# Padded rows for the split x: where a matmul's moving operand begins

## The chip, the core and the metric

The kernel runs on one core of a Trainium2 chip. A core has five engines with queues of their own: TensorE (PE in the profile; its weight loads are PEld) multiplies matrices into PSUM, VectorE (DVE) and ScalarE (ACT) work elementwise, GpSimd (POOL) does a few elementwise and power operations, and SyncE (SP) issues transfers. On-chip memory (SBUF) has 128 partitions; an address below is a byte within a partition. The metric is the device time of one execution in microseconds (us); the time before is the median of three runs.

## What is computed

One layer of an encoder: the stream h is 16 meta tokens ahead of 1024 positions (T = 1040), width 1024. A combined projection of the normalized stream feeds a bidirectional retention with 4 heads and a windowed attention with 8 heads; both are gated, projected, merged, projected once more, normalized and added to h. Cut to what matters:

```python
u = _rms_norm(h, pre_w)
z = u @ w_in
rq, rk, rv, rg, aq, ak, av, ag, gr, ga = _split_in(z)
o_r = _bidirectional_retention(rq, rk, rv, lg_f, lg_b)
o_r = group_norm(o_r) * ret_nw * silu(rg)
y_r = o_r @ w_rb
o_a = _windowed_sink_attention(aq, ak, av, sink) * silu(ag)
y_a = o_a @ w_ab
mix = sigmoid(gr) * y_r + sigmoid(ga) * y_a
return h + _rms_norm(mix @ w_o, post_w)
```

## The kernel before

Everything that a matmul multiplies is split into a high part, rounded to float32r, and a low part, the remainder; `mm3` (line 73) makes a product of three matmuls, high by high, low by high and high by low. In the profile these are lines 75, 76 and 77.

**x.** The transposed stream times the norm's weight is kept split for the whole kernel in the four tiles `big[s][i]` (line 132): s = 0 is the high part, s = 1 the low part, i the upper or lower four of the eight rows k. A row k holds 128 of the 1024 input channels on the partitions and all T = 1040 columns, so rows lie 4160 bytes apart. Columns 0 to 15 are the meta tokens, columns 16 to 527 and 528 to 1039 the two halves. `proj` (line 136) uses x as the moving operand, in slices of 512 columns (`HALVES`, for queries) or 256 and 272 (`PIECES`, for keys), with the weights as the stationary one. `projT` (line 156) has x as the stationary operand and moves 256 columns of weights, for the values; for the 16 meta rows it uses `xm` instead, a packed copy that `pack_meta` makes. The profile names x `big` in all these places.

**Stages.** First comes the set-up: eight matmuls on zeros (`idle`, line 310) ahead of the first data, then the first head's query and key projection. Then four retention heads, with the next head's projections as filler between; decay tables `DT` are made a head ahead by `decay_table` (line 244) from `tabt`, in the loop over chunks c of `retention`. Attention follows, in 32 chunks, with query and key projections and some gate products (`pe`) as filler; its scores are combined with `mask` (line 1375 of the profile).

**The Strassen phases.** The gate projections (z, 16 units of 256 output channels) and the last three matrix products (r, a and o, 4 units each) use Strassen's scheme with seven products of half size. A product p of a unit u is 12 matmuls of 512 columns: three for each of four rows k. `PROD` gives its operands: the left one is a piece of the weights or a sum of pieces, made by `prepare` six products ahead; the right one stands in `B` for the whole phase. B11, B21, B22 and T1 are the quarters of `big` (the two halves of columns by the two halves of rows). T2, T3 and T4 are tiles of their own with rows of 2048 bytes, named T in the profile. Products 1, 2, 3 and 5 stream from `big`, products 4, 6 and 7 from T4, T2 and T3. Some products are made early and left out of a unit's list. Between two phases `refill` writes the next phase's right operands into the same places: `split_b` (line 917) with one operation on ScalarE and one on VectorE to a row, or `get_pre` (line 1090) with transfers of parts made earlier. T4 of the last phase comes by `get_pre` on SP.

The order of work on each engine is written out by hand through `fill`, `issue_after` and the tables of hooks, and set by the order in which the calls are recorded. The pools lay out SBUF from the bottom: tiles of the pool `keep` first, `big` among them.

Of the kernel before, what the change touches and what calls it, by code (L numbers as in the profile page):

```python
# [14 lines left out]
NM = 16  # L15
# [4 lines left out]
NH = 4  # L20
# [2 lines left out]
PIECES = [(0, 272), (272, 528), (528, 784), (784, 1040)]  # L23
HALVES = [(16, 528), (528, 1040)]
MW = 416
FILL = (9, 9, 7, 7, 7, 7, 6, 6), (7,) * 8, (7, 6, 6, 6, 6, 6, 6, 5), (5, 5, 5, 5, 5, 5, 8)
PRE = {u: (2, 3) if u > 5 else (2,) for u in range(2, 14)}

# [10 lines left out]
def block_kernel(ctx: ExitStack, tc: tile.TileContext, x0, xT, x, meta, w_in, w_rb, w_ab, w_out, post_w,  # L39
# [33 lines left out]
    def mm3(o, ah, al, bh, bl, first, last, free_group=False):  # L73
        kw = {"skip_group_check": True} if free_group else {}
        nc.tensor.matmul(o, ah, bh, start=first, stop=False, **kw)  # L75
        nc.tensor.matmul(o, al, bh, start=False, stop=False, **kw)  # L76
        latest[:] = [nc.tensor.matmul(o, ah, bl, start=False, stop=last, **kw).ins]  # L77
        return latest[0]
# [11 lines left out]
    def dve_lo(o, i, hi):  # L90
        return nc.vector.tensor_tensor(o, i, hi.bitcast(F32), ALU.subtract).ins  # L91
# [5 lines left out]
    rcol = keep.tile([P, 9], F32, name="rcol")  # L97
    rbc = keep.tile([P, T], F32, name="rbc")
    rnw = keep.tile([P, KT], F32, name="rnw")
    mhalf = keep.tile([P, 24], F32, name="mhalf")  # L100
    nc.vector.memset(mhalf, -0.5)

    def fetch_w(src, u):
# [25 lines left out]
            split(t, act)  # L129
        return w  # L130

    big = [[keep.tile([P, 4, T], R, name=f"big{i}_{s}") for i in range(2)] for s in range(2)]
    xh = [big[0][k // 4][:, k % 4] for k in range(KT)]
    xl = [big[1][k // 4][:, k % 4] for k in range(KT)]

    def proj(w, m0, a, b, name):
        wh, wl = w
# [6 lines left out]
        return t  # L144


    xm = wp.tile([P, KT, 2 * 32], R, name="xm")
    nc.vector.memset(xm.bitcast(F32), 0.0)

    def pack_meta():  # L150
        for i in range(2):
            for s in range(2):
                t = nc.vector.tensor_copy(xm[:, 4 * i:4 * i + 4, 32 * s:32 * s + NM], big[s][i][:, :, 0:NM].bitcast(F32))
        return t.ins

    def projT(w, c, name, mt=None):
# [39 lines left out]


    DT = ra.tile([P, NH, P], F32, name="DT")
    tabt = ra.tile([P, 3 * P], F32, name="tabt")
    mask = ra.tile([P, MW], F32, name="mask")  # L200
    warm = ra.tile([P, 1], F32, name="warm")
    neg, na, e, e2, s_, ss, acc, lg = (ra.tile([P, 8], F32, name=n) for n in (
        "neg", "na", "e", "e2", "s_", "ss", "acc", "lg"))
# [40 lines left out]
    def decay_table(hs):  # L244
        for h in hs:
            t = ra.tile([P, P], F32, tag="rw", bufs=3, name=f"dd{h}")
            nc.vector.tensor_scalar(t, tabt[:, 2 * P:3 * P], lg[:, 4 + h:5 + h], None, op0=ALU.mult)
            nc.vector.scalar_tensor_tensor(t, tabt[:, P:2 * P], lg[:, h:h + 1], t, op0=ALU.mult, op1=ALU.add)
            nc.scalar.activation(DT[:, h], t, AF.Exp)
# [17 lines left out]
    with tc.tile_pool(name="setup", bufs=1, reuse_waits="tile") as st:  # L267
# [32 lines left out]
            nc.sync.dma_start(xr[k], xT[k])  # L300
        nc.sync.dma_start(cr, rope[0])
        nc.sync.dma_start(sr, rope[1])
        nc.sync.dma_start(tabt, tab[:, MW:])
        w0 = tuple((lambda k, a, b, l=l: l[k // 4][:, k % 4, a:b]) for l in wt)


        idle = pj("idle")
        zeros = xm.rearrange("p k e -> p (k e)")
        for i in range(8):
            nc.tensor.matmul(idle, zeros[:, 0:P], zeros, start=True, stop=True)  # L310


        outs = [(P, a, b, t(f"pk0_{a}")) for (a, b), t in zip(PIECES, (pj, pj, p1, p3))]
# [68 lines left out]
        normed = nc.vector.tensor_tensor(kdr[:, 0:NH, 0], r2[:, 0:1].to_broadcast([P, NH]), dtab[:, 16:20], ALU.mult).ins  # L382
    nc.gpsimd.tensor_tensor(rcol, ms, mhalf[:, 0:9], ALU.pow)
    nc.vector.tensor_copy(ident, tabt[:, 0:P])
    nc.sync.dma_start(mask, tab[:, 0:MW])

    def row_factors():

# [52 lines left out]
    def retention(h, fill, begin=lambda: None):  # L441
# [98 lines left out]
        for c in range(9):  # L540
            if 0 < c < 8:
                stage1(c + 1)
            if c == 1:
                while pend:
                    pend.pop(0)()
            if h == 0 and c == 4:
                pins.extend((state["v"], state["vl"], state["S"]))
            if h == NH - 1 and c == 1:
                pre_fetch(6)
            if h == NH - 1 and c == 2:  # L550
                with tc.issue_after(state["vl"]):
                    pre_sums(6)
            if h == NH - 1 and c in (4, 6):
                fill(KT)
            if h == NH - 1 and 1 < c < 6:
                with tc.issue_after(state["vl"]):
                    turn_factors(*PIECES[c - 2])
            if h < NH - 1 and c == 4:
                with tc.issue_after(state["vl"]):
                    decay_table((h + 1,))  # L560
            if h == 1 and c == 2:
                row_factors()
            stage2(c)
# [329 lines left out]
    with follow(*latest):  # L893
# [5 lines left out]


    half = [slice(NM, NM + 512), slice(NM + 512, T)]
    B = {"B11": [big[s][0][:, :, half[0]] for s in range(2)], "T1": [big[s][0][:, :, half[1]] for s in range(2)],
         "B21": [big[s][1][:, :, half[0]] for s in range(2)], "B22": [big[s][1][:, :, half[1]] for s in range(2)]}
    PROD = {1: ("A11", "B11"), 2: ("A12", "B21"), 3: ("S4", "B22"), 4: ("A22", "T4"), 5: ("S1", "T1"),
            6: ("S2", "T2"), 7: ("S3", "T3")}
    free = ["pj"] * 3
    POST = {2: (0, 0), 7: (1, 1), 3: (0, 1), 4: (1, 0)}
    final = "o", 3, 4
    sub, mul, add = ALU.subtract, ALU.mult, ALU.add
# [5 lines left out]
        return gp.tile([P, 512], F32, tag="g", bufs=6, name=name)  # L915

    def split_b(n, k, src):
        h, l = B[n]
        nc.scalar.copy(h[:, k], src)
        dve_lo(l[:, k], src, h[:, k])  # L920

    class Phase:
        def __init__(self, nm, seq, load, post, fetch=None, apart=(), early=(), pre={}):
# [64 lines left out]
        def product(self, u, p):  # L988
            if (self.nm, u, p) == final:
                return self.last_product(u, p)  # L990
            st = self.u.setdefault(u, {})
            at = {1: "X", 6: "X", 7: "W" if u in self.apart else "X", 5: "Y", 3: "V" if u in self.early or (self.nm, u) == final[:2] else "Y", 2: "Z",
                  4: "W" if u in self.apart else "X"}[p]
            new = at not in st
            if new:
                b = free.pop(0)
                st[at] = bank(b, f"b{self.nm}{u}_{p}"), b
            t = st[at][0]
            h, l = self.ops.pop((u, p))
            bh, bl = B[PROD[p][1]]  # L1000
            for k in range(4):
                mm3(t, h[:, k], l[:, k], bh[:, k], bl[:, k], new and k == 0, k == 3, True)
            self.combine(u, p, st)

        def last_product(self, u, p):

            h, l = self.ops.pop((u, p))
            bh, bl = B[PROD[p][1]]
            o = self.u[u]["u3"]
            for a in (0, 256):  # L1010
                t = bank(free.pop(0), f"b{self.nm}{u}_{p}_{a}")
                s = slice(a, a + 256)
                for k in range(4):
                    mm3(t[:, 0:256], h[:, k], l[:, k], bh[:, k, s], bl[:, k, s], k == 0, k == 3)
# [74 lines left out]

    def get_pre(n):  # L1090
        for s in range(2):
            nc.sync.dma_start(B[n][s].bitcast(F32), pre_d[n][s])

    def get_sum(n):
        for k in range(4):
# [190 lines left out]
    def square(r, m2, c, o):  # L1286
        m1 = rows[r][2]
        jk = gtile(f"jk{r}_{c}")
        nc.scalar.activation(jk[:, 0:o.shape[1]], o, AF.Square, accum_out=m2[:, c:c + 1])
        if not m1:  # L1290
            m1.append(gp.tile([P, 1], F32, tag="ms1", bufs=6, name=f"ms1_{r}"))
            nc.vector.tensor_scalar(m1[0], m2[:, c:c + 1], 0.25 / D, EPS, op0=ALU.mult, op1=ALU.add)
        else:
            nc.vector.scalar_tensor_tensor(m1[0], m2[:, c:c + 1], 0.25 / D, m1[0], op0=ALU.mult, op1=ALU.add)
# [43 lines left out]
    def attention():  # L1338
# [4 lines left out]
        def stage1(hp, n):  # L1343
# [19 lines left out]
            for e_ in range(2):  # L1363
                hd = 2 * hp + e_
                if (hp, e_, i) not in aqs:
                    split_q(hp, e_, i)
                a_, b_ = (t[:, o0:o0 + P] for t in aqs[hp, e_, i])
                s = p2(f"ps{hd}_{n}")
                mm3(s[:, 0:wid], a_, b_, kh[:, start:start + wid], kl[:, start:start + wid], True, True)
                if n == 0:  # L1370
                    if hp:
                        raw[e_] = aw.tile([P, 401], F32, tag=f"raw{e_}", bufs=1, name=f"raw{hd}")
                    nc.vector.tensor_copy(raw[e_][:, 0:1], nsink[:, hd:hd + 1])
                p = pp[:, e_]
                nc.vector.tensor_tensor_reduce(raw[e_][:, 1:1 + wid], s[:, 0:wid], mask[:, mo:mo + wid], -SCALE,  # L1375
                                               nsink[:, hd:hd + 1], ALU.add, ALU.min, nm_[:, e_:e_ + 1])
# [169 lines left out]
    free.extend(["p1", "p1", "p2", "p2", "p3"])  # L1546
    yp, gp, yt = (ctx.enter_context(tc.tile_pool(name=n, bufs=1, reuse_waits="tile")) for n in ("yp", "gp", "yt"))
    for n in ("T2", "T3", "T4"):
        B[n] = [yt.tile([P, 4, 512], R, name=f"{n}{s}")[:, :, :] for s in range(2)]
    for n in ("T2", "T3", "T4"):  # L1550
        get_sum(n)
        next(steps)
# [79 lines left out]
```

## Time and profile before

| | us |
|---|---|
| median of three runs | 1053.21 (1052.04 to 1054.81) |
| the profiled execution | 1053.81 |
| its span, first to last instruction | 1051.7 |

The stages, with the busy time of TensorE and VectorE and the mean busy share of the 16 DMA engines in each stretch:

| stretch, us | what runs | PE | DVE | DMA |
|---|---|---|---|---|
| 5 to 29 | set-up, head 0's projection | 23.77 | 19.77 | 1.02 |
| 90 to 331 | retention heads | 241.00 | 181.81 | 0.30 |
| 331 to 440 | attention, first part | 108.96 | 81.70 | 0.57 |
| 440 to 555 | attention, second part | 114.12 | 86.23 | 0.58 |
| 555 to 620 | z phase, first part | 64.86 | 59.80 | 0.80 |
| 740 to 803 | z phase, last part | 63.00 | 56.23 | 0.58 |
| 803 to 881 | r phase | 77.65 | 71.11 | 0.60 |
| 881 to 960 | a phase | 78.77 | 64.88 | 0.86 |
| 960 to 1045 | o phase | 85.00 | 56.34 | 0.56 |

Matmuls overlap: the next starts while the one before is still in the array, so a matmul's duration in the profile (about 0.39 us at 512 columns) is longer than the distance to the next start. What a stretch of matmuls costs is read from the starts. In a row of a view by groups stand the line, the engine, the operation, the tiles written and read, the shape, the count, and then the busy time in us, the mean duration in ns and the idle time ahead. Buffer numbers are left out of the names.

### The profile page before, as it was taken

The numbers are of one execution on the slowest core, as the hardware profiler recorded it, in microseconds if no ns is written. First come the engines' busy times: TensorE is split into PE (matmuls) and PEld (weight loads), VectorE is DVE, ScalarE is ACT, GpSimd is POOL, SyncE is SP. The second block draws the span as 40 slices with busy tenths as digits, with TensorE's granted clock in tenths as the row PEclk, the third lists the DMA queues.
The fourth block names the chain that finished last, engine by engine and source line by source line (L and its number), as shares of the span: only waits on it lengthen the run. The fifth ranks groups of instructions, "written<-read, shape, count | busy, mean of one in ns | idle before, by whom it ended". The sixth has DMA issues, their size and how long they took to land. (4 is left out here: it accounts for less than half of the span.)

```text
span 1051.7 us, 17222 instructions
## 1 busy us (share of the span) xinstructions
PE 1040.9 (99%) x5880; PEld 905.4 (86%) x5880; DVE 838.3 (80%) x1788; ACT 506.5 (48%) x1127; POOL 228.4 (22%) x338
## 2 busy tenths in 40 slices
PE   9999999999999999999999999999999999999997
PEld 8998999989989888988888888778888788788886
DVE  6876758768875777777769988998899899778665
ACT  5631432423423566665667544555556446334443
POOL 3445244243242333443310000000000000111032
PEclk9999999999999999999999999999999999999999
DMA  9433223243231466666549678999935747789464
GB/s 347 176 86 87 65 46 83 69 92 98 77 92 61 101 176 182 174 183 168 161 154 347 188 255 318 306 321 345 394 106 170 256 154 233 224 232 315 126 120 80
DMA packets 96758, 188.43 MB, mean 179 GB/s; under 512 B 10944, under 2 KB 35552, under 8 KB 95856
## 3 DMA queue, kind: packets, MB, share of 16 engines
q1 hardware_dynamic: 79120, 162.89, 46.1%
q0 software_dynamic: 10176, 14.73, 9.4%
q10 hardware_dynamic: 7376, 9.73, 2.6%
q8 instruction: 46, 0.75, 0.3%
q14 instruction: 40, 0.33, 0.1%
HBM read 124.32 MB, written 57.68 MB: 173 GB/s over the span
## 5 line engine op out<-in xcount | busy, mean ns | idle before, releaser
L1247 POOL DMA_DIRECT2D mx_d<-c1a x4 | 3.6, 890 | 398.7 <-DVE c1a L1238 379.7
L76 PE MATMUL bz<-T,llz 128*128 128x512 f32 x192 | 75.0, 391 | 0.0
L77 PE MATMUL bz<-T,lhz 128*128 128x512 f32 x192 | 74.8, 389 | 0.0
L75 PE MATMUL bz<-T,lhz 128*128 128x512 f32 x192 | 74.5, 390 | 0.2 <-DVE u2z L1028 0.2
L76 PE MATMUL pv<-wh,big 128*128 128x256 f32 x256 | 73.2, 286 | 0.0
L75 PE MATMUL pv<-wh,big 128*128 128x256 f32 x256 | 73.2, 286 | 0.0
L77 PE MATMUL pv<-wl,big 128*128 128x256 f32 x256 | 73.1, 286 | 0.0
L76 PE MATMUL bz<-big,llz 128*128 128x512 f32 x176 | 69.7, 396 | 0.1
L75 PE MATMUL bz<-big,lhz 128*128 128x512 f32 x176 | 68.8, 395 | 0.6 <-ACT lhz L943 0.5
L77 PE MATMUL bz<-big,lhz 128*128 128x512 f32 x176 | 69.3, 394 | 0.0
L1378 ACT ACTIVATE p<-raw,nm 128x401 f32<-128x401 f32 (+1 forms) x64 | 38.3, 600 | 32.8 <-DVE nm L1375 31.5
L1388 POOL TENSOR_SCALAR p<-p,den 128x400 f32<-128x400 f32 (+1 forms) x60 | 37.6, 684 | 68.4 <-DVE den L1381 64.8
L75 PE MATMUL paq<-big,wh 128*128 128x512 f32 x128 | 51.8, 404 | 0.0
L76 PE MATMUL paq<-big,wl 128*128 128x512 f32 x128 | 50.8, 397 | 0.0
L77 PE MATMUL paq<-big,wh 128*128 128x512 f32 x128 | 50.4, 394 | 0.0
L75 PEld LDWEIGHTS pv<-wh,big 128*128 128x128 f32 x256 | 48.2, 188 | 0.4
L76 PEld LDWEIGHTS pv<-wh,big 128*128 128x128 f32 x256 | 48.2, 188 | 0.4
L77 PEld LDWEIGHTS pv<-wl,big 128*128 128x128 f32 x256 | 48.3, 189 | 0.3
L91 DVE TENSOR_TENSOR wl<-wr,wh 128x1024 fp32r<-128x1024 f32 x28 | 34.8, 1247 | 10.9 <-POOL wh L88 6.8
L75 PEld LDWEIGHTS bz<-T,lhz 128*128 128x128 f32 x192 | 36.0, 188 | 8.4 <-DVE u2z L1028 0.6
L76 PEld LDWEIGHTS bz<-T,llz 128*128 128x128 f32 x192 | 36.0, 188 | 8.0 <-DVE llz L91 0.3
L77 PEld LDWEIGHTS bz<-T,lhz 128*128 128x128 f32 x192 | 36.1, 188 | 7.6
(616 smaller groups left out, 3603.5 us busy)
## 6 DMA issues: line engine op xcount, KB each, us to landing
wrz<-in_w_in_dram SPq DMA_DIRECT2D x32, 512.0 KB, 6.2
wr<-in_w_in_dram SPq DMA_DIRECT2D x29, 512.0 KB, 3.8
we<-in_w_in_dram SPq DMA_DIRECT2D x16, 512.0 KB, 4.2
tg<-tg_d SPq DMA_DIRECT2D x32, 256.0 KB, 5.0
T<-preT SPq DMA_DIRECT2D x6, 1024.0 KB, 8.2
e<-e ACTq DMA_DIRECT2D x20, 256.0 KB, 2.9
e<-e SPq DMA_DIRECT2D x20, 256.0 KB, 4.9
xn<-in_x_dram SPq DMA_DIRECT2D x8, 512.0 KB, 9.2
```

The source lines that it names most:

```text
L75: nc.tensor.matmul(o, ah, bh, start=first, stop=False, **kw)
L76: nc.tensor.matmul(o, al, bh, start=False, stop=False, **kw)
L77: latest[:] = [nc.tensor.matmul(o, ah, bl, start=False, stop=last, **kw).ins]
L91: return nc.vector.tensor_tensor(o, i, hi.bitcast(F32), ALU.subtract).ins
L1247: nc.gpsimd.dma_start(d, to, accum_op=ALU.add)
L1378: last["exp"] = nc.scalar.activation(p[:, 0:1 + wid], raw[e_][:, 0:1 + wid], AF.Exp, scale=-1.0, bias=nm_[:, e_:e_ + 1], accum_out=den[:, ...
L1388: nc.gpsimd.tensor_scalar(pt[e_][:, 0:wid], pt[e_][:, 0:wid], den[:, e_:e_ + 1], 1.0, op0=ALU.mult, op1=ALU.mult)
```

## The change

- The four tiles of x become two, `big[s]`, with eight rows of LEFT + T = 1088 columns, 4352 bytes. x stands in columns 48 to 1087; columns 0 to 47 of each row are padding. `mhalf` grows by 64 bytes, which moves the start of `big`.
- T4 loses its fourth row (k = 3). It goes into `margins`: the padding and the 16 meta columns of all eight rows, 8 pieces of 64 columns. `right(n, s, k)` returns the operand and a function that views a flat row as 8 by 64. `product`, `last_product` and `split_b` go through it; `get_pre` brings the row by a transfer of its own for each part.
- `mask` takes the buffer of `tabt` and is loaded in retention head 2, behind the last decay table, instead of in the set-up.
- `xm` has 48 columns a row instead of 64, and the idle matmuls stream 384 columns instead of 512.
- `ms1` has 4 buffers instead of 6.

```diff
+LEFT = 48
...
-    mhalf = keep.tile([P, 24], F32, name="mhalf")
+    mhalf = keep.tile([P, 40], F32, name="mhalf")
...
-    big = [[keep.tile([P, 4, T], R, name=f"big{i}_{s}") for i in range(2)] for s in range(2)]
-    xh = [big[0][k // 4][:, k % 4] for k in range(KT)]
-    xl = [big[1][k // 4][:, k % 4] for k in range(KT)]
+    big = [keep.tile([P, KT, LEFT + T], R, name=f"big{s}") for s in range(2)]
+    xh, xl = ([b[:, k, LEFT:LEFT + T] for k in range(KT)] for b in big)
...
-    xm = wp.tile([P, KT, 2 * 32], R, name="xm")
+    xm = wp.tile([P, KT, 32 + NM], R, name="xm")
...
-    tabt = ra.tile([P, 3 * P], F32, name="tabt")
-    mask = ra.tile([P, MW], F32, name="mask")
+    tabt = ra.tile([P, MW], F32, tag="tb", bufs=1, name="tabt")
...
-            nc.tensor.matmul(idle, zeros[:, 0:P], zeros, start=True, stop=True)
+            nc.tensor.matmul(idle[:, 0:KT * (32 + NM)], zeros[:, 0:P], zeros, start=True, stop=True)
...
-    nc.sync.dma_start(mask, tab[:, 0:MW])
+    mask = []
+
+    def load_mask():
+        mask.append(ra.tile([P, MW], F32, tag="tb", bufs=1, name="mask"))
+        nc.sync.dma_start(mask[0], tab[:, 0:MW])
...
             if h < NH - 1 and c == 4:
                 with tc.issue_after(state["vl"]):
                     decay_table((h + 1,))
+                if h == NH - 2:
+                    load_mask()
...
-    B = {"B11": [big[s][0][:, :, half[0]] for s in range(2)], "T1": [big[s][0][:, :, half[1]] for s in range(2)],
-         "B21": [big[s][1][:, :, half[0]] for s in range(2)], "B22": [big[s][1][:, :, half[1]] for s in range(2)]}
+    B = {n: [big[s][:, 4 * i:4 * i + 4, LEFT + half[j].start:LEFT + half[j].stop] for s in range(2)]
+         for n, i, j in (("B11", 0, 0), ("T1", 0, 1), ("B21", 1, 0), ("B22", 1, 1))}
...
+    margins = [b[:, :, 0:LEFT + NM] for b in big]
+
+    def right(n, s, k):
+        if n == "T4" and k == 3:
+            return margins[s], lambda t: t.rearrange("p (a c) -> p a c", a=KT)
+        return B[n][s][:, k], lambda t: t
...
     def split_b(n, k, src):
-        h, l = B[n]
-        nc.scalar.copy(h[:, k], src)
-        dve_lo(l[:, k], src, h[:, k])
+        (h, as_), (l, _) = (right(n, s, k) for s in range(2))
+        nc.scalar.copy(h, as_(src))
+        dve_lo(l, as_(src), h)
...
             for k in range(4):
-                mm3(t, h[:, k], l[:, k], bh[:, k], bl[:, k], new and k == 0, k == 3, True)
+                (bh, as_), (bl, _) = (right(PROD[p][1], s, k) for s in range(2))
+                mm3(as_(t), h[:, k], l[:, k], bh, bl, new and k == 0, k == 3, True)
...
+                    if k == 3:
+                        c = slice(a // 64, a // 64 + 4)
+                        mm3(t[:, 0:256].rearrange("p (a c) -> p a c", a=4), h[:, k], l[:, k], bh[:, c], bl[:, c],
+                            False, True)
...
         for s in range(2):
-            nc.sync.dma_start(B[n][s].bitcast(F32), pre_d[n][s])
+            m = B[n][s].shape[1]
+            nc.sync.dma_start(B[n][s].bitcast(F32), pre_d[n][s][:, 0:m])
+            if m < 4:
+                d, as_ = right(n, s, m)
+                nc.sync.dma_start(d.bitcast(F32), as_(pre_d[n][s][:, m]))
...
-            m1.append(gp.tile([P, 1], F32, tag="ms1", bufs=6, name=f"ms1_{r}"))
+            m1.append(gp.tile([P, 1], F32, tag="ms1", bufs=4, name=f"ms1_{r}"))
...
-        B[n] = [yt.tile([P, 4, 512], R, name=f"{n}{s}")[:, :, :] for s in range(2)]
+        B[n] = [yt.tile([P, 3 if n == "T4" else 4, 512], R, name=f"{n}{s}")[:, :, :] for s in range(2)]
```

More of the change, by code (lines that the diff above doesn't have):

```diff
@@ L152, in pack_meta @@
             for s in range(2):
-                t = nc.vector.tensor_copy(xm[:, 4 * i:4 * i + 4, 32 * s:32 * s + NM], big[s][i][:, :, 0:NM].bitcast(F32))
+                t = nc.vector.tensor_copy(xm[:, 4 * i:4 * i + 4, 32 * s:32 * s + NM],
+                                          big[s][:, 4 * i:4 * i + 4, LEFT:LEFT + NM].bitcast(F32))
         return t.ins
@@ L302, in block_kernel @@
         nc.sync.dma_start(sr, rope[1])
-        nc.sync.dma_start(tabt, tab[:, MW:])
+        nc.sync.dma_start(tabt[:, 0:3 * P], tab[:, MW:])
         w0 = tuple((lambda k, a, b, l=l: l[k // 4][:, k % 4, a:b]) for l in wt)
@@ L999, in product @@
             h, l = self.ops.pop((u, p))
-            bh, bl = B[PROD[p][1]]
             for k in range(4):
-                mm3(t, h[:, k], l[:, k], bh[:, k], bl[:, k], new and k == 0, k == 3, True)
+                (bh, as_), (bl, _) = (right(PROD[p][1], s, k) for s in range(2))
+                mm3(as_(t), h[:, k], l[:, k], bh, bl, new and k == 0, k == 3, True)
             self.combine(u, p, st)
@@ L1007, in last_product @@
             h, l = self.ops.pop((u, p))
-            bh, bl = B[PROD[p][1]]
             o = self.u[u]["u3"]
@@ L1013, in last_product @@
                 for k in range(4):
-                    mm3(t[:, 0:256], h[:, k], l[:, k], bh[:, k, s], bl[:, k, s], k == 0, k == 3)
+                    (bh, _), (bl, _) = (right(PROD[p][1], e_, k) for e_ in range(2))
+                    if k == 3:
+                        c = slice(a // 64, a // 64 + 4)
+                        mm3(t[:, 0:256].rearrange("p (a c) -> p a c", a=4), h[:, k], l[:, k], bh[:, c], bl[:, c],
+                            False, True)
+                    else:
+                        mm3(t[:, 0:256], h[:, k], l[:, k], bh[:, s], bl[:, s], k == 0, False)
                 with tc.high_priority(200):
@@ L1374, in stage1 @@
                 p = pp[:, e_]
-                nc.vector.tensor_tensor_reduce(raw[e_][:, 1:1 + wid], s[:, 0:wid], mask[:, mo:mo + wid], -SCALE,
+                nc.vector.tensor_tensor_reduce(raw[e_][:, 1:1 + wid], s[:, 0:wid], mask[0][:, mo:mo + wid], -SCALE,
                                                nsink[:, hd:hd + 1], ALU.add, ALU.min, nm_[:, e_:e_ + 1])
```

## The prediction

> **What bounds the kernel now.** I read the page first for how full each engine is, then the list of what TensorE waited for, then the matmuls one by one in the order of time.
>
> ```profile
> PE 1040.9 (99%) x5880; PEld 905.4 (86%) x5880; DVE 838.3 (80%) x1788; ACT 506.5 (48%) x1127; POOL 228.4 (22%) x338
> ...
> PE idle L310 <- DVE warm L208: 1.5, 1, 1.5
> PE bz L75 <- ACT lhz L943: 0.5, 1, 0.5
> ```
>
> TensorE (PE) is busy 1040.9 of 1051.7 us. In the list of waits (in all, times, longest, in us) the longest is the 1.5 us ahead of the first instruction; the next is 0.5 us. So no other engine and no transfer holds the path for long: the time is the sum of the distances from one matmul's start to the next one's. A busy share can't say whether these distances are as short as they can be, since the ends are modelled; the starts can. The view in order of time, TensorE alone (start, duration in us, line), gives whole products of 12 matmuls, of which I keep the first row and the row that follows the last:
>
> ```profile
> 613.83 0.39 PE L75 MATMUL bz<-T,lhz 128*128 128x512 f32 x1
> ...
> 616.55 0.39 PE L75 MATMUL bz<-T,lhz 128*128 128x512 f32 x1
> ...
> 638.73 0.39 PE L75 MATMUL bz<-T,lhz 128*128 128x512 f32 x1
> ...
> 641.47 0.39 PE L75 MATMUL bz<-T,lhz 128*128 128x512 f32 x1
> ...
> 789.28 0.39 PE L75 MATMUL bz<-big,lhz 128*128 128x512 f32 x1
> ...
> 789.96 0.40 PE L75 MATMUL bz<-big,lhz 128*128 128x512 f32 x1
> ...
> 790.66 0.40 PE L75 MATMUL bz<-big,lhz 128*128 128x512 f32 x1
> ...
> 791.37 0.40 PE L75 MATMUL bz<-big,lhz 128*128 128x512 f32 x1
> ...
> 792.07 0.39 PE L75 MATMUL bz<-big,lhz 128*128 128x512 f32 x1
> ```
>
> The same work, with the same 128x512 shape, the same kind of stationary operand and no wait in it, takes 2.72 and 2.74 us when its moving operand comes from a T tile, and 2.79 us when it comes from big. The last five rows show where the difference sits: a product runs over four rows k of its operand, three matmuls to a row (L75 to L77). Row 0 takes 0.68 us, as a T row does (2.72 / 4); rows 1 to 3 take 0.70, 0.71 and 0.70 us.
>
> What sets row 0 of big apart is its address. A row of a big tile is T = 1040 columns, 4160 bytes, which is 64 modulo 256; in the built program the tiles begin at 64 modulo 256, and both halves begin 64 bytes (or 64 + 2048) into a row. So rows 0 to 3 begin at 128, 192, 0 and 64 modulo 256. All T rows are 2048 bytes from a base at 128. One start of the four, 128, is the fast one; that 0 is no better than 64 I take from the rows as they are, without a reason for it.
>
> The groups by shape (count, busy us, mean ns) show that this holds in every stage; of each I keep line 77, whose counts are those of 75 and 76 too:
>
> ```profile
> L77 PE MATMUL bz<-T,lhz 128*128 128x512 f32 x192 | 74.8, 389 | 0.0
> L77 PE MATMUL bz<-big,lhz 128*128 128x512 f32 x176 | 69.3, 394 | 0.0
> L77 PE MATMUL paq<-big,wh 128*128 128x512 f32 x128 | 50.4, 394 | 0.0
> L77 PE MATMUL pe<-big,weh 128*128 128x512 f32 x80 | 31.5, 394 | 0.0
> L77 PE MATMUL ba<-big,lha 128*128 128x512 f32 x64 | 25.2, 394 | 0.0
> L77 PE MATMUL pq<-big,wh 128*128 128x512 f32 x48 | 18.9, 394 | 0.0
> ```
>
> 394 ns for every group on big, 389 on T.
>
> **The change, part by part.** *The rows (term 1).* Rows become 1088 columns, 4352 = 17 x 256 bytes, the tiles begin at 128 modulo 256, and the data begin 48 columns in: every 512-column start is then 128 modulo 256, as in T. The big groups count 176 + 128 + 80 + 3 x 64 + 48 + 16 = 640 on each of three lines, 1920 matmuls (br and bo have ba's 4 units x 4 products on big x 4 rows = 64; head 0's queries 2 halves x 8 rows = 16, as each of the three heads in pq). The four Strassen phases (bz, br, ba, bo) have 1104 of them, 92 products. From the rows above a big product takes 2.79 us, a T product 2.73 on the mean of two: 0.06 x 92 = 5.5 us. The projections (paq, pe, pq) have 816, 68 times twelve. Two such twelves of head 3:
>
> ```profile
> 215.56 0.39 PE L75 MATMUL pq<-big,wh 128*128 128x512 f32 x1
> ...
> 218.36 0.39 PE L75 MATMUL pq<-big,wh 128*128 128x512 f32 x1
> ...
> 221.85 0.39 PE L75 MATMUL pq<-big,wh 128*128 128x512 f32 x1
> ...
> 224.63 0.39 PE L75 MATMUL pq<-big,wh 128*128 128x512 f32 x1
> ```
>
> 2.80 and 2.78 us, again 2.79: 0.06 x 68 = 4.1 us. Together 9.6 us. The least that these rows allow is 2.78 - 2.74 = 0.04 for all 160, 6.4 us; the most 2.80 - 2.72 = 0.08, 12.8 us. The group means give 5 ns x 1920 = 9.6 us as well. With 2.785 us as the typical product (between 2.78 and 2.79) it is 0.055 x 160 = 8.8; I take 9.2, half way.
>
> The Trainium skill, "TensorE: Matmul & The Clock Gate" (section "Wait — 56ns, not 53.3ns?"), gives the distance of warm matmuls as columns / 2.4 GHz plus some 2.5 ns, 215.7 ns at 512 columns, with no term for an address. The trace's 2720 / 12 = 227 ns and 2790 / 12 = 232 ns agree neither with it nor with each other; by that rule term 1 is nothing.
>
> *Matmuls of 256 columns and less.* Their starts move too (the chunks of the retention's tiles from 192 to 0 modulo 256, the weights as moving operands stay). Two groups of four in a row, on different operands:
>
> ```profile
> 301.69 0.28 PE L76 MATMUL pa<-vh,sl 128*128 128x256 f32 x1
> ...
> 302.17 0.28 PE L77 MATMUL pa<-Slf,qh 128*128 128x256 f32 x1
> ...
> 1042.02 0.28 PE L75 MATMUL bo<-T,lho 128*128 128x256 f32 x1
> ...
> 1042.50 0.28 PE L76 MATMUL bo<-T,llo 128*128 128x256 f32 x1
> ```
>
> 0.48 us for four in both, although the first begin at 192 (vh, Slf) and the second at 128. So at 256 columns the start shows no price, and I take nothing.
>
> *T4's fourth row in the margins (term 2).* Product 4 now streams row 3 of T4 as 8 pieces of 64 columns, 4352 bytes apart: 28 units x 3 = 84 matmuls (in the last one two half-width triples). No row of the trace has a moving operand in pieces. Bounds: at best a piece costs nothing, since each begins at 128 modulo 256 and the output stays one run of 512. At worst a new piece restarts the stream as a new matmul does: two 256-column matmuls take 0.24 us against 0.227 for one of 512, 13 ns a restart, 7 restarts x 84 x 13 = 7.6 us. In between lies the price of one slow start, 5 ns a matmul, 0.4 us; I take that, because the piece has neither a new stationary operand nor a new output.
>
> *The warm-up (term 3).* xm shrinks from 64 to 48 columns a row, so the eight idle matmuls stream 384 columns instead of 512.
>
> ```profile
> 1.48 3.78 PE L310 MATMUL idle<-xm 128*128 128x512 f32 x8 [1.48 <-DVE warm L208]
> 5.49 0.77 PE L75 MATMUL pq<-big,w 128*128 128x512 f32 x1 [0.23 <-ACT big L330]
> 6.05 0.63 PE L76 MATMUL pq<-big,w 128*128 128x512 f32 x1
> 6.48 0.41 PE L75 MATMUL pk<-big,w 128*128 128x272 f32 x1
> ...
> 7.08 0.40 PE L75 MATMUL pq<-big,w 128*128 128x512 f32 x1
> ```
>
> Until 6.48 us a 512-column matmul takes 0.43 us (6.05 to 6.48) and shows 0.63 us of duration; at 7.08 it shows the 0.40 of all later rows. So full speed comes about 5.0 us after the first idle matmul. The idle ones now end 8 x 0.43 / 4 = 0.86 us sooner, while the first real one still waits for ScalarE's high part of x at 5.49: TensorE has that much more of a hole. If full speed comes later by the hole, half of it is lost, 0.4 us; at worst the 5.0 us run again at half speed, 2.5 us; at best nothing. I take 0.4. The Trainium skill (same page, "What's actually happening") has the clock decided per free-running window of 3.41 us of activity; a window missed would cost an estimated 1.7 us, inside these bounds, and no run here shows the window.
>
> *The mask.* It now uses tabt's buffer and is asked for on SP behind VectorE's last read of the tables.
>
> ```profile
> L248 DVE SCALAR_TENSOR_TENSOR dd<-tabt,lg,dd x4: 330/347/349, 43.1 to 189.8; 128x128 f32<-128x128 f32 x4
> 186.63 5.62 SPq L580 DMA_DIRECT2D oTr_d<-ost  x2
> L1375 DVE CUSTOM_DVE_ANT_0 raw<-ps,mask,nsink x64: 491/630/636, 336.9 to 545.7; 128x400 f32<-128x400 f32 x48, 128x272 f32<-128x272 f32 x16
> ```
>
> The last table read ends at 190.1 us. Queued behind the new wait on SP is the second of these two output chunks, which goes at about 192 by itself (186.63 + 5.62, less its own issue), and behind that the weights of the next head; SP therefore stands there anyway. The first reader of the mask comes at 336.9, 145 us later. Cost nothing; without that cover, the attention's first chunk would wait for one landing.
>
> *T4's reload ahead of phase o* becomes four transfers, two of them in pieces of 256 bytes.
>
> ```profile
> 959.05 0.39 PE L75 MATMUL bo<-big,lho 128*128 128x512 f32 x1
> 967.59 0.79 SPq L1092 DMA_DIRECT2D T<-preT  x2
> ```
>
> Phase o begins at 959.05 and T4 is the operand of its 13th product: 12 x 2.73 us later, at 992 at the earliest, 24 us after the request. Two more issues of 0.4 us and pieces of 256 bytes don't fill that. Nothing; a reload later than that would hold this product. The instructions' order on every engine stays that of before, but for a few dozen matmuls of the first 25 us; TensorE gets 19 more waits on its own finished matmuls, each over 100 matmuls old, so they are met on arrival. The two ms1 buffers fewer add no wait of VectorE that comes late. Nothing for these.
>
> *What the others make of a faster TensorE (term 4).* Busy us of the engines in a stretch (PE, PEld, DVE, ACT, POOL, then clock and DMA share):
>
> ```profile
> 680.00:740.00 60.00, 59.72 (x259) 48.01 (x258) 55.45 (x92) 31.14 (x54) 0.00 (x0) 1.00 0.97 340
> ```
>
> In this stretch of the z phase VectorE is 92% busy and the DMA engines 97%. TensorE gets about 1% shorter there, which both can still follow on the mean. At worst all that z gains is lost: 44 products x 0.06 = 2.6 us; I take 0.4.
>
> *Sum:* 9.2 - 0.4 - 0.4 - 0.4 = 8.0 us less. The profiled execution took 1053.81 us (span 1051.7, 2.1 around it), which gives 1045.8; it lies 0.6 above the median of the three runs, 1053.21, so the median becomes 1045.2.
>
> **The rivals.** (a) *The others eat part of it:* z's gain is lost to VectorE and DMA (2.6), and the clock comes as late as its bound (2.5): 9.2 - 0.4 - 2.6 - 2.5 = 3.7 less, 1049.5. For it: 92% and 97%; against it: no wait of TensorE above 0.5 us in the list. (b) *The pieces cost 13 ns a restart:* 9.2 - 7.6 - 0.8 = 0.8 less, 1052.4. For it: the price that a new matmul has; against it: nothing else is new in a piece. (c) *The start isn't the cause:* something else sets row 0 and T apart, and the time stays, 1053.2; this is also what the skill's formula gives. Against it: row 0 of big shares only its start with T, not the row's length nor its tile; T's rows 1 to 3 are as fast as its row 0. (d) *Slower:* a piece restarts the stream at the price that short matmuls have.
>
> ```profile
> 500.85 0.62 PE L1405 MATMUL pt<-ident,p 128*128 128x128 f32 x4
> ```
>
> Four of 128 columns take 0.62 us with a tail of some 0.27, 0.115 each, where a quarter of 227 ns is 57: 58 ns a restart, 588 restarts, 34 us: 1053.2 - 8.4 + 34 = 1079. It decides from 14 ns a restart, where it has eaten the 8.4 us of the rest. Those are transposes of another type of data, which speaks against it.
>
> **How the numbers follow.** The forecast has 0.75, with a range of its own of 1042.6 to 1048; (a) 0.08, (b) 0.06, (c) 0.04, (d) 0.07. The range must leave out (b), (c) and (d) at most: 1042.6, where term 1 is nearly 11 us and nothing is given back, to 1050.5, which holds (a). This kernel's runs differ by 0.3% (3.2 us), so that is what can be told from no change: faster by more 0.83 (forecast and (a)), within it 0.10 ((b) and (c)), slower 0.07 ((d)).
>
> **What would show it.** Right: the big groups of 512 columns at 389 to 390 ns, big products 2.72 to 2.74 us from start to start, all four rows alike; TensorE's waits as short as before. Term 2: the third line of T4's row 3 in the bz products at 0.23 us to the next start, or longer by the restarts. Term 3: the idle group at about 2.9 us for eight, and the row from which 512 columns show 0.40. Term 4: new waits on VectorE or DMA between 555 and 803 us. I am wrong if the big groups stay at 394, or if product 4 is longer than the others.

## The result, and the profile after

| | before | after |
|---|---|---|
| median of 10 runs each, us | 1053.66 (1052.04 to 1055.84) | 1050.81 (1049.72 to 1053.56) |
| the profiled execution, us | 1053.81 | 1049.72 |
| its span, us | 1051.7 | 1047.6 |

The ratio is 0.9975, with an interval of 0.9964 to 0.9986: faster by 2.85 us of median, where the prediction had 8.0. The profiled execution of after is the fastest of its ten runs, so the two traces are 4.1 us apart and the medians 2.85.

The line of busy times on the page of after:

```profile
PE 1032.9 (99%) x5880; PEld 906.8 (87%) x5880; DVE 838.9 (80%) x1788; ACT 505.6 (48%) x1127; POOL 227.1 (22%) x338
```

TensorE is busy 8.0 us less than before (1040.9), but the span is only 4.1 us shorter, so part of what it gained it now stands idle. Where, is read in three views. First the order of time on TensorE (start, duration, line), in the z phase; `mm3` is now on lines 76 to 78, and of each product of 12 I keep the first row:

```profile
735.50 0.39 PE L76 MATMUL bz<-big,lhz 128*128 128x512 f32 x1
...
738.22 0.39 PE L76 MATMUL bz<-T,lhz 128*128 128x512 f32 x1
...
740.94 0.39 PE L76 MATMUL bz<-T,lhz 128*128 128x512 f32 x1
...
742.98 0.39 PE L76 MATMUL bz<-big,lhz 128*128 128x512 f32 x1
...
743.66 0.39 PE L76 MATMUL bz<-big,lhz 128*128 128x512 f32 x1
```

A product on big (735.50), one on T (738.22) and one on T4 (740.94, its last three matmuls on the margins from 742.98) all take 2.72 us; the three on the margins take 0.68, a quarter of it. So x streams as fast as T, and the 8 pieces of T4's fourth row cost nothing. The groups by shape say the same of every stage:

```profile
L78 PE MATMUL bz<-big,lhz 128*128 128x512 f32 x192 | 74.2, 389 | 0.0
...
L78 PE MATMUL pv<-wl,big 128*128 128x256 f32 x256 | 73.5, 287 | 0.0
...
L78 PE MATMUL paq<-big,wh 128*128 128x512 f32 x128 | 50.1, 392 | 0.0
...
L78 PE MATMUL ba<-big,lha 128*128 128x512 f32 x68 | 26.5, 389 | 0.0
...
L78 PE MATMUL pq<-big,wh 128*128 128x512 f32 x48 | 18.7, 390 | 0.0
```

The groups of 512 columns on big went from 394 to 389 in the Strassen phases and to 390 to 392 ns in the projections. The second row is one of 256 columns: pv's high-by-low line had 286 ns before and has 287 now. That looks like nothing, but there are 1040 such matmuls of pv and pav, and the starts show it better. Here are the first and the 25th matmul of 24 in a row in the first values of head 0, before and then after:

```profile
30.61 0.28 PE L75 MATMUL pv<-wh,big 128*128 128x256 f32 x1
...
33.45 0.28 PE L75 MATMUL pv<-wh,big 128*128 128x256 f32 x1
```

```profile
30.77 0.28 PE L76 MATMUL pv<-wh,big 128*128 128x256 f32 x1
...
33.64 0.28 PE L76 MATMUL pv<-wh,big 128*128 128x256 f32 x1
```

24 of them took 2.84 us and now take 2.87. From all starts of the two traces (stalls, more than 25 ns over the median of their kind, left out), the mean distance went from 118.0 to 119.2 ns for the 1040 of pv and pav, from 117.6 to 119.3 for the 432 of pk and pak, and from 118.6 to 119.2 for the 740 of retention and attention on their own tiles: 1.3 + 0.7 + 0.4 = 2.4 us lost. For 512 columns it went from 232.4 to 228.8 ns in the 816 of the projections (2.9 us) and, over the 2100 of the Strassen phases, from 483.0 to 476.3 us in all (6.7 us): 9.6 us gained. Of the 6.7 us, 0.8 came on T, whose starts did not change (227.6 to 226.8 ns).

The third view is TensorE's waits (in all, times, longest, in us) of after, its six largest:

```profile
PE pq L76 <- ACT big L330: 1.6, 2, 1.1
PE idle L310 <- DVE warm L208: 1.4, 1, 1.4
PE bz L77 <- DVE llz L92: 1.1, 1, 1.1
PE ba L77 <- DVE lla L92: 0.9, 1, 0.9
PE br L77 <- DVE llr L92: 0.8, 2, 0.6
PE bz L76 <- ACT lhz L956: 0.5, 1, 0.5
```

The first row is the set-up: the shorter idle group ends sooner, so TensorE waits 1.1 us for the first part of x, which it begins at 5.40 us (5.49 before), and 0.5 us for another at 9.02; the first values of head 0 begin 0.16 us later than before (30.77 for 30.61). Before, nothing after the start was longer than 0.5 us. Now TensorE waits in z, a and r for VectorE's low part of the left operand (llz, lla, llr), up to 1.1 us at a time. The busy times over the four Strassen phases (555 to 1045 us before, 555 to 1040 after; the sum over the phases, then the mean) give its size:

```profile
sum 490.00, PE 488.47 PEld 397.40 DVE 420.14 ACT 246.42 POOL 26.21; mean PE 122.12 PEld 99.35 DVE 105.04 ACT 61.60 POOL 6.55
```

```profile
sum 485.00, PE 481.52 PEld 396.72 DVE 419.40 ACT 246.04 POOL 26.20; mean PE 120.38 PEld 99.18 DVE 104.85 ACT 61.51 POOL 6.55
```

TensorE was idle there for 490.00 - 488.47 = 1.5 us and now is for 485.00 - 481.52 = 3.5 us. From the starts the stalls in these phases went from 3.5 to 5.5 us. Both say 2.0 us more.

So the trace accounts for -9.6 + 2.4 + 2.0 = -5.2 us, against -4.1 of span; the 1.1 us between are for the most part short stalls elsewhere (among the keys' matmuls 0.7, among those of 128 columns 0.6), which I don't explain further.

### The profile page after: what moved, and what is told of

Read it like the earlier page. It is cut to its first block, busy times and chain, and to the rows that moved or that the text cites. A ratio compares the mean times of both kernels' runs of the same rounds, so it can differ in the third digit from the quotient of the medians.

```text
span 1047.6 us, 17241 instructions
## 1 busy us (share of the span) xinstructions
PE 1032.9 (99%) x5880; PEld 906.8 (87%) x5880; DVE 838.9 (80%) x1788; ACT 505.6 (48%) x1127; POOL 227.1 (22%) x338
## 5 line engine op out<-in xcount | busy, mean ns | idle before, releaser
L77 PE MATMUL bz<-big,llz 128*128 128x512 f32 x192 | 74.8, 390 | 0.1
L76 PE MATMUL bz<-big,lhz 128*128 128x512 f32 x192 | 74.1, 390 | 0.5 <-ACT lhz L956 0.5
L78 PE MATMUL bz<-big,lhz 128*128 128x512 f32 x192 | 74.2, 389 | 0.0
L77 PE MATMUL bz<-T,llz 128*128 128x512 f32 x176 | 68.6, 390 | 1.1 <-DVE llz L92 1.1
L78 PE MATMUL bz<-T,lhz 128*128 128x512 f32 x176 | 68.5, 389 | 0.0
L76 PE MATMUL bz<-T,lhz 128*128 128x512 f32 x176 | 68.0, 389 | 0.0
L76 PEld LDWEIGHTS bz<-big,lhz 128*128 128x128 f32 x192 | 36.0, 188 | 8.6 <-ACT lhz L956 1.3
L77 PEld LDWEIGHTS bz<-big,llz 128*128 128x128 f32 x192 | 36.0, 188 | 7.9 <-DVE llz L92 0.5
L78 PEld LDWEIGHTS bz<-big,lhz 128*128 128x128 f32 x192 | 36.0, 188 | 7.5
```

## The experiments

All start from the changed kernel. Two questions are open: why do 256 columns get slower when x begins at 128, and is the new idle time in the Strassen phases really a consequence of TensorE's pace?

**x at the other three starts.** `mhalf` sets where big begins, a tile behind big keeps all that follows where it was. Only x moves, to 64, 192 or 0 modulo 256; T and all weights stay at 128.

```diff
-    mhalf = keep.tile([P, 40], F32, name="mhalf")
+    mhalf = keep.tile([P, 24], F32, name="mhalf")
...
+    keep.tile([P, 16], F32, name="shift")
```

(56 and 48 columns for 192, 72 and 32 for 0.)

> The changed kernel, with x alone begun at 64 modulo 256 instead of 128 (all other tiles keep their start modulo 256). Theory A (a width has its own good start: 128 for 512 columns, others for 256): matmuls of 512 columns on big go from 227 ns start to start to 233, all four rows alike, and a product of 12 from 2.72 to 2.80 us; those of 256 columns that move x (pk) or hold it (pv) go from 120 ns back to 117 or 118. Theory B (256 columns take 120 ns wherever every row begins alike, because nothing breaks the rhythm): 512 as in A, but pk and pv stay at 120. A gives 1050.8 + 1920 x 6 ns - 1270 x 2.5 ns = 1059; B gives 1062.

> The same with x begun at 192 modulo 256. Theory A: 512 columns at 232 to 233 ns, pk and pv at 118. Theory B: pk and pv at 120. A product of 12 takes 2.78 to 2.80 us in both.

> The same with x begun at 0 modulo 256. Theory A: 512 columns at 232 to 234 ns, pk and pv at 118 to 119. Theory B: pk and pv at 120. A product of 12 takes 2.79 to 2.82 us in both.

s64 took 1055.36 us (1054.5 to 1056.59, 10 runs), a ratio of 1.0013 [1.0003, 1.0022] to before; s192 took 1050.85 and s0 1055.72 in one run each. In order of time, the first rows of 24 matmuls of pv and of a product on big, each with the row that follows the last one; s64 and then s192:

```profile
31.52 0.28 PE L76 MATMUL pv<-wh,big 128*128 128x256 f32 x1
...
34.35 0.28 PE L76 MATMUL pv<-wh,big 128*128 128x256 f32 x1
...
779.32 0.39 PE L76 MATMUL bz<-big,lhz 128*128 128x512 f32 x1
...
782.12 0.39 PE L76 MATMUL bz<-big,lhz 128*128 128x512 f32 x1
```

```profile
31.99 0.28 PE L76 MATMUL pv<-wh,big 128*128 128x256 f32 x1
...
34.71 0.28 PE L76 MATMUL pv<-wh,big 128*128 128x256 f32 x1
...
778.40 0.39 PE L76 MATMUL bz<-big,lhz 128*128 128x512 f32 x1
...
781.15 0.40 PE L76 MATMUL bz<-T,lhz 128*128 128x512 f32 x1
```

At 64 the product takes 2.80 us and the 24 take 2.83; at 192 it is 2.75 and 2.72. So 512 columns did get slow at 64, as both theories said, but at 192 they got half as slow as both said, and the time of s64 lay below both (1059 and 1062), where TensorE's stalls in the Strassen phases fell from 5.5 us in after to 2.8. Of 256 columns theory A had pv in s64 right (117.5 ns on the mean) and no more: pv, whose *moving* operand is the weights and did not move at all, went from 2.87 to 2.83 and 2.72 us. What moved is its stationary operand, x. pk, which has x as the moving operand, went the other way round: 115.9 ns in s64 and 117.4 in s192. Width alone, or evenness of the starts, doesn't give this. That led to theory C: what counts is the difference between the start of the moving and that of the stationary operand, modulo 256.

**The weights instead of x.** nsink, at the end of SBUF, sets where the split weights of the projections and the left operands of the Strassen phases begin; here at 64, with x and T still at 128.

```diff
-    nsink = edge.tile([P, 24], F32, name="nsink")[:, 0:8]
+    nsink = edge.tile([P, 40], F32, name="nsink")[:, 0:8]
```

> The changed kernel, with the split weights (the tiles of wp and the later lh and ll) begun at 64 modulo 256 instead of 128; x stays at 128. They are the moving operand of pv and pav (256 columns, 1040 matmuls) and the stationary one of pk, pq, paq, pe and of all Strassen products. Theory A1 (only the moving operand's start counts): pv and pav go from 120 to 117 ns, all else stays, some 3 us less than the changed kernel: 1048. Theory A2 (what counts is that moving and stationary operand begin alike): 512 columns lose their 227 ns and go to 232, 13 us more on 2900 matmuls: 1063. Theory B: nothing moves, 1050.8.

It took 1049.1 us (1048.04 to 1050.27, 5 runs), a ratio of 0.9953 [0.9939, 0.9967].

```profile
31.36 0.28 PE L76 MATMUL pv<-wh,big 128*128 128x256 f32 x1
...
34.09 0.28 PE L76 MATMUL pv<-wh,big 128*128 128x256 f32 x1
...
779.59 0.39 PE L76 MATMUL bz<-T,lhz 128*128 128x512 f32 x1
...
782.34 0.39 PE L76 MATMUL bz<-T,lhz 128*128 128x512 f32 x1
```

Each theory had a part of it. The product of 512 columns, here on T, takes 2.75 us, neither 2.72 nor 2.79, although no moving operand of 512 columns was touched: the stationary operand's start counts, as A2 said, though at 229 ns and not at 232. pv went to 2.73 us for 24, a little below what A1 had.

**Both by the same step.** If the difference counts, nothing may change when both paddings do.

```diff
-    nsink = edge.tile([P, 24], F32, name="nsink")[:, 0:8]
+    nsink = edge.tile([P, 40], F32, name="nsink")[:, 0:8]
...
-    mhalf = keep.tile([P, 40], F32, name="mhalf")
+    mhalf = keep.tile([P, 24], F32, name="mhalf")
```

> The changed kernel with both paddings changed (24 columns ahead of the rows of x, 40 ahead of the split weights), so that x, T and all split weights and operands of TensorE begin 64 bytes lower, at 64 modulo 256; no start changes against another one. Theory C (the difference between the moving and the stationary operand's start decides): 512 columns stay at 227 ns, 256 columns at 119 to 120, and the time is that of the changed kernel, 1049.5 to 1052. Theory of the prediction (the moving operand's own start decides, and 128 is the fast one): 512 columns back at 232 to 233 ns, 2900 of them by 5.5 ns are 16 us, and the time is over 1060.

1051.5 us (1049.47 to 1052.39, 10 runs), a ratio of 0.9975 [0.9965, 0.9986], the same as that of the change itself.

```profile
31.41 0.28 PE L76 MATMUL pv<-wh,big 128*128 128x256 f32 x1
...
34.28 0.28 PE L76 MATMUL pv<-wh,big 128*128 128x256 f32 x1
...
777.43 0.39 PE L76 MATMUL bz<-big,lhz 128*128 128x512 f32 x1
...
780.15 0.39 PE L76 MATMUL bz<-big,lhz 128*128 128x512 f32 x1
```

The same 2.87 and 2.72 us as after, with x at 64 as in s64, where a product took 2.80; the time over 1060 that the prediction's theory gives did not come. So moving both starts by 64 has no effect, and the difference between them does. From all starts of the traces (stalls left out), with the 512 columns taken from the Strassen phases:

| moving start minus stationary start, modulo 256 | 512 columns, ns | product of 12, us | 256 columns, ns |
|---|---|---|---|
| 0 | 226.8 (after, all64) | 2.72 | 119.2 to 119.3 (after: pv, pk, own tiles) |
| +64 | 228.9 (w64), 230.0 (s192) | 2.75 | 117.4 to 117.6 (s192 pk, w64 pk, s64 pv) |
| -64 | 233.3 (s64) | 2.80 | 115.5 to 115.9 (s64 pk, s192 pv, w64 pv) |
| 128 | 232.8 (s0) | 2.80 | 118.5 (s0 pk, pv) |

For 256 columns the table also gives the mean of the kernel before. There x's rows stood at all four differences in turn, a quarter of pv and pk at each; the mean of the last column is 117.7 ns, and 117.6 (pk) and 118.0 (pv) were seen. For 512 columns it does not: the mean of the second column is about 230.6 ns, and 232.4 (projections) and 232.2 (big in the Strassen phases) were seen. A row at +64 took 0.70 us there (the second of the four in the prediction) and takes 0.69 in s192, where all rows are alike.

Three things stay open. The table holds where every matmul of a stretch has the same difference; what a mixture costs is not derived from it. In the projections of after, also at 0, the mean is 228.8 and not 226.8 ns. And a stationary operand is loaded while other matmuls run (PEld is busy for 906.8 us beside 1032.9 of PE); since all partners in a stretch begin alike, these runs can't tell whether the difference to a matmul's own stationary operand counts or that to the next one's.

**The Strassen phases alone at the old pace.** A gap at the end of their pool moves the left operands, nothing else; the four phases run at a difference of -64.

```diff
+    lp.tile([P, 48], F32, name="lgap")
     yp, gp, yt = (ctx.enter_context(tc.tile_pool(name=n, bufs=1, reuse_waits="tile")) for n in ("yp", "gp", "yt"))
```

> The changed kernel with a gap of 192 bytes behind the right-hand pool of the Strassen phases, so that their split stationary operands begin at 192 modulo 256 and the 2100 moving operands of 512 columns there (big and T) begin 64 bytes below them; nothing else moves. By the difference table these go from 227 to 233 ns, 6.4 ns each, 13.4 us more TensorE work in the phases z, r, a, o. Theory W (part of a faster TensorE goes into waits for VectorE and ScalarE there): the time that TensorE waits in these phases falls from 5.5 to about 3 us and the kernel loses about 11 us: 1061.5. Rival (the waits don't depend on TensorE's pace): the whole 13.4 us, 1064.2.

1059.98 us (1059.36 to 1060.24, 4 runs), a ratio of 1.0062 [1.0046, 1.0079] to before, and 9.2 us more than after. A product, all of str's waits on TensorE, and the sums of its busy times in the windows of after:

```profile
781.60 0.39 PE L76 MATMUL bz<-big,lhz 128*128 128x512 f32 x1
...
784.40 0.39 PE L76 MATMUL bz<-big,lhz 128*128 128x512 f32 x1
```

```profile
PE idle L310 <- DVE warm L208: 1.4, 1, 1.4
PE pq L76 <- ACT big L330: 1.2, 1, 1.2
PE bz L76 <- ACT lhz L956: 0.5, 1, 0.5
PE pt L1427 <- POOL p L1410: 0.3, 1, 0.3
PE pt L1432 <- DVE pbl L92: 0.3, 1, 0.3
```

```profile
sum 485.00, PE 484.34 PEld 389.26 DVE 413.08 ACT 243.80 POOL 20.70; mean PE 121.08 PEld 97.32 DVE 103.27 ACT 60.95 POOL 5.17
```

The product takes 2.80 us, and the waits for llz, lla and llr (2.8 us in the list of after) are gone; of the same stretch of 485 us TensorE is idle for 0.7 instead of 3.5. From the starts, its matmuls took 13.7 us more (476.3 to 490.0) and the stalls fell from 5.5 to 1.3 us, 9.5 us net. Theory W holds: nothing but TensorE's pace was changed, and 4.2 of 13.7 us, three in ten, were taken up by waits, most of them for VectorE. One of them, in r after the change:

```profile
820.34 0.40 PE L76 MATMUL br<-T,lhr 128*128 128x512 f32 x1
...
821.33 0.50 PE L77 MATMUL br<-T,llr 128*128 128x512 f32 x1 [0.59 <-DVE llr L92]
```

The matmul on the high part starts at 820.34, the one on the low part only at 821.33, where 0.23 us later would have been due.

**A better start for 256 columns.** Four kernels give the matmuls of 256 columns the difference -64 while 512 columns in the Strassen phases keep 0. vwh: the high halves of the V weights alone (48 columns into a wider buffer; `vmeta` has one buffer instead of two to make room, in all four kernels). own: gaps between the tiles of retention and attention (`gap` lays out an unused tile of so many columns once). best: both. ownw: own, and the weights as in w64, with the gap of str so that the Strassen phases stay at 0.

```diff
+        o = 48 if U_V <= u < U_G or u == U_AV else 0
+        t = wp.tile([P, 1024 + 64], R, tag="wh", bufs=4, name=name)
+        return t[:, o:o + 1024].rearrange("p (k c) -> p k c", k=4)
...
+                gap(rp, 16, "gk" + d)
                 a = rp.tile([P, P], R, tag="kh" + d, bufs=2, name=f"kh{d}{h}_{c}")
...
+            gap(rp, 48, "gs")
             a = rp.tile([P, 256], R, tag="Sh", bufs=2, name=f"Sh{nm}")
...
+            gap(ap, 48, "gp0")
             ah = ap.tile([P, 512], R, tag="pah", bufs=2, name=f"pah{hp}_{n}")
```

> The changed kernel with the high halves of the V weights alone begun at 64 modulo 256 instead of 128 (all other weights stay at 128, the low halves of V too), so that 640 matmuls of 256 columns (512 pv, 128 pav) have a moving operand that begins 64 bytes below the stationary one modulo 256, and the 320 with low halves do not. Theory C: those 640 go from 119-120 to 115-116 ns, their neighbours with low halves and all of 512 columns stay, and 640 by 3.6 ns give 2.3 us: about 1048.5. Rival (the stages in which pv runs are paced by other engines): the matmuls get faster, the time stays within 0.5 us of 1050.8.

> The changed kernel with gaps of 16 or 48 columns between the tiles of retention and attention, so that their own 256-column matmuls (pa, pb, pkv, po without the meta one, 720 in all) have a moving operand that begins 64 bytes below the stationary one modulo 256. Theory C: 119 to 115.5 ns each, 2.5 us in all, 1048.3. Rival (these matmuls lie between waits for other engines, which take the gain): within 0.5 us of 1050.8.

> The two edits to 256-column operands together (the high halves of V and the own tiles of retention and attention), 512 columns as in the changed kernel. Theory C: the sum of both, 4.8 us, about 1046. If only one of them pays, 1048.4; if neither, 1050.8.

> The gaps of own, and besides all split weights of the projections at 64 modulo 256 (x and T stay at 128, the operands of the Strassen phases too): pv and pav get a moving operand 64 bytes below the stationary one with high and low halves alike, pk, pak and the 512 columns of pq, paq and pe one 64 bytes above. By the difference table against own: 1040 by -3.6 ns, 432 by -1.7 ns, 816 by +2.2 ns: 2.7 us less TensorE work, 1045.0. Rival (in the stages of retention and attention the gain of own is all that the other engines leave): 1047.6 or, with the 1.8 us that 512 columns lose, up to 1049.

| | time, us | runs | ratio to before |
|---|---|---|---|
| vwh | 1049.67 (1048.68 to 1051.47) | 4 | 0.9957 [0.9940, 0.9973] |
| own | 1047.60 (1046.55 to 1048.56) | 4 | 0.9935 [0.9920, 0.9951] |
| best | 1047.90 (1047.14 to 1050.38) | 6 | 0.9944 [0.9929, 0.9959] |
| ownw | 1047.61 (1046.16 to 1050.23) | 6 | 0.9945 [0.9931, 0.9960] |

All four have a lower median than the change; for own, best and ownw the intervals end at 0.9960 or below, and the change's begins at 0.9964. vwh's is not told apart from it, and best, where the sum of both gains was expected (1046), took no less than own. `vmeta`'s single buffer is in all four and was not tried alone. In vwh, 24 matmuls of pv in a row:

```profile
32.01 0.28 PE L76 MATMUL pv<-wh,big 128*128 128x256 f32 x1
...
34.87 0.28 PE L76 MATMUL pv<-wh,big 128*128 128x256 f32 x1
```

2.86 us, where two thirds of them at -64 and one third at 0 should have given 2.77 (two thirds of the 2.72 of s192 and a third of the 2.87 of after). Over all 1040 the mean is 118.4 ns, not 117. A difference that changes within the chain lost most of the gain here; the expectation of vwh was wrong there. In own the tiles of retention and attention fell from 119.2 to 117.1 ns, 1.6 us of the 2.5 expected. The profiled executions of own and after are 1.2 us apart (1048.56 and 1049.72), no more than the starts give; the medians are 3.2 us apart, which is more, so part of own's lead is not explained. ownw's starts do show most of what was expected of it (pv and pav 116.2 ns, pk and pak 117.7, 512 columns of the projections 229.6), its span is the shortest of all at 1044.1, but the median isn't below own's: 1047.61, as its rival had it. Its waits show where a part is lost:

```profile
PE bz L76 <- DVE u2z L1054: 1.4, 1, 1.4
...
PE bz L77 <- DVE llz L92: 0.9, 2, 0.6
PE ba L77 <- DVE lla L92: 0.9, 1, 0.9
PE br L77 <- DVE llr L92: 0.8, 2, 0.6
```

TensorE reaches z earlier (549.6 us against 554.9 after) and waits more there, for a combination on VectorE (u2z) too; its stalls in the Strassen phases are 7.5 us. One more thing keeps these sums from being read finer: the set-up ends at another time in each run. The first pv matmul with x starts between 30.17 us (ownw) and 32.55 us (str) in the traces, although the set-up's order is the same in all.

## Why the prediction was wrong

- **Term 1, the rows: right in its sum, in part by luck.** Predicted 9.2 us from 1920 matmuls; measured 9.6 from the starts, with every undisturbed product of the Strassen phases at 2.72 us. The parts were off in opposite ways: the projections gave 2.9 us where 4.1 were priced, and the Strassen phases 6.7 where 5.5 were, 0.8 of them on T, which the sum left out. And its reading, "One start of the four, 128, is the fast one", was right by chance: 128 is fast because the stationary operands stand at 128 (s64 and all64 have x at the same start and differ by 0.08 us a product).
- **"Matmuls of 256 columns and less": the first step that failed.** It took nothing, from two chains of four at 0.48 us whose moving operands begin at 192 and 128. By the addresses in the built program the stationary operands of these chains begin at 192 and 128 as well: both have difference 0, and the comparison could not show what counts. The matmuls that the change did touch are pv, pav, pk and pak, with x on one side or the other; they went from a mixture of four differences to 0, the best one for 512 columns and the worst for 256. That cost 2.0 us. The own tiles of retention and attention lost 0.4 more, although their difference is 0 in both kernels. Nor is it their start: in all64 they begin at 192 again, as before, and still take 119.2 ns; in s64, s192, s0 and w64, where they stand as in after and only x or the weights were moved, they take 118.6 to 118.8. So they go with the matmuls around them; how is open.
- **Term 4, what the others make of a faster TensorE: the second step, mis-sized.** Taken as 0.4 us with a bound of 2.6, because the list of waits was empty; measured 2.0, and str shows that it is this mechanism. The row it rested on had VectorE 92% busy in z and was priced for z alone; the waits came in a too (0.2 to 0.9 us for lla), where VectorE was 82% busy. A list of waits almost empty said only that TensorE was late enough at its old pace.
- **Term 2, T4's row in pieces: 0.4 taken, 0 measured.** Rivals (b) and (d), which have a piece restart the stream, fall with it (742.98 to 743.66 above).
- **Term 3, the warm-up: 0.4 taken, no loss from the clock measured.** The idle group now takes 2.93 us, as said, but 512 columns show the 0.40 us of full speed from 5.71 us on, earlier than before:

```profile
1.36 2.93 PE L310 MATMUL idle<-xm 128*128 128x384 f32 x8 [1.36 <-DVE warm L208]
...
5.71 0.40 PE L77 MATMUL pq<-big,w 128*128 128x512 f32 x1
```

- **The mask, T4's reload, the order: nothing**, as said. No wait for them stands in the list of after.
- **Rival (a)** named the right direction, a part eaten by VectorE, and put it at 1049.5. It came near by luck: 2.5 us of its price were for the clock, which cost nothing, and the 2.4 us of the 256 columns took their place. The range that was built on it ended at 1050.5, just below 1050.81. Rival (c), that the start isn't the cause, is refuted for 512 columns by str and s64. The Trainium skill, "TensorE: Matmul & The Clock Gate" (section "Wait — 56ns, not 53.3ns?"), gives one distance for a number of columns; these runs don't agree, with 226.8 to 233.3 ns for 512.

Sum of the steps with what was measured: 9.6 - 2.4 - 0 - 0 - 2.0 = 5.2 us in place of 8.0. Less the 1.1 us of short stalls elsewhere, these are the 4.1 us by which the two traces differ; the medians differ by 2.85, since the profiled execution of after is its fastest, and what sets the others apart from it no trace shows.

## What to carry to other kernels

Before an operand is moved to a better start, list every matmul that has it on either side, moving and stationary, with the start of its partner: here the partner decided, and the best difference for 512 columns was the worst for 256. Price an apparent tie from starts over 24 or more matmuls in a row, since 1 ns on 2200 matmuls is 2 us. And where a second engine is nearly as busy as the one that gets faster (here VectorE, 82 to 92% busy), don't price its waits from a list that is almost empty: here they took three tenths of the gain, in the change (2.0 of 6.7 us) and in str (4.2 of 13.7).

## What the runs showed of the hardware that was not expected

- Where a whole stretch has one difference, the distance between float32r matmuls goes with moving start minus stationary start modulo 256, and in opposite senses by width: 226.8 to 233.3 ns at 512 columns (best at 0, worst at -64), 115.5 to 119.3 at 256 (best at -64, worst at 0).
- Mixing differences within a chain took most of the gain: 2.86 us for 24 in vwh, against 2.73 in w64, where all stand at -64, and 2.77 for the mixture by its parts.
- A moving operand in 8 pieces of 64 columns, 4352 bytes apart, streams as fast as one of 512 in a row: 0.68 us for three.
